# Where the row-chunk sums of layer 0's modulation vectors 2 to 5 are taken: VectorE accumulators in place of TensorE products

## The chip, the core and the metric

The kernel runs on one core of a Trainium2 chip (trn2). Its engines work side by side, each through its own queue in order: TensorE (PE; PEld is its weight load) multiplies 128x128 blocks into PSUM, VectorE (DVE) and ScalarE (ACT) work on tiles of 128 partitions, GpSimd (POOL) does a few small operations, and SyncE (SP) issues nearly all loads. The metric is device microseconds of one execution; the median of three runs before the change is 2529.5 us.

## The reference, cut to what matters

Two transformer layers and a second block work on 512 tokens of 1024 features; layer 0 also carries 256 context tokens. Each layer is modulated by six vectors that come from the conditions c (tokens) and c_ctx (context):

```python
silu_c = jax.nn.silu(c)
silu_cc = jax.nn.silu(c_ctx)
for layer in range(DEPTH):
    mod_x = jnp.split((silu_c @ ada_w[layer] + ada_b[layer])[:, None, :], 6, axis=-1)
    mod_c = jnp.split((silu_cc @ ada_w[layer] + ada_b[layer])[None, None, :], 6, axis=-1)
    hx = rms_norm(x, norm1_g[layer]) * (1 + mod_x[1]) + mod_x[0]
    ...                                       # the mixer: y_x, y_c
    x = x + mod_x[2] * y_x
    x = x + mod_x[5] * sqrelu_mlp(rms_norm(x, norm2_g[layer]) * (1 + mod_x[4]) + mod_x[3], mlp_w1[layer], mlp_w2[layer])
    ...                                       # the same for the context in layer 0
```

A vector i is thus two rows (for c and c_ctx) times a matrix of 1024 x 1024, 4 MB of ada_w. Vectors 0 and 1 of layer 0 are needed at the start; vector 2 after the mixer, 3 and 4 at the second norm, 5 at the end of the feed-forward.

## The kernel before

Activations lie feature-major, eight chunks of 128 features by 512 tokens, split into two parts hi and lo so that a product of full precision is three matmuls (line 302 in fm, feature-major; line 332 in tm, token-major). A unit of 256 weight columns is loaded on SP (line 262) and split by ScalarE and VectorE (lines 339, 340).

Layer 0 runs so. A start-up with an order written out by hand (to about 76 us) makes vectors 0 and 1 chunk by chunk together with the norm and the first product. Then come two token-major products (to 112 us), the gate scans of the mLSTM on VectorE (lines 748 to 763, whose results TensorE transposes in line 769), eight feature-major products (to 259 us: "the projections"), the mLSTM head by head (259 to about 380 us) and the output product, whose first weights are staged through two tiles named ada (line 245). In the mLSTM TensorE makes scores (lines 852 to 862), ScalarE their exponentials e (line 204), VectorE the products r = scores times e (line 869), and TensorE the outputs from r (line 884); lines 888 to 896 are the short end of a query tile, 901 to 910 that of a head. The scores run three tiles ahead of the outputs of the group before.

Vectors 2 to 5 of layer 0 are mixed into this as "fillers": generators of which pump() takes one step at certain places, one after each of the ten products and two in each group of queries of the mLSTM. ada(l, i) has eight steps for a vector. Each loads 128 rows by 1024 columns of ada_w (512 KB, line 472) into one of two tiles ada and lets line 464 multiply them by the conditions: four matmuls of 32 columns of weights side by side, accumulated in one PSUM tile over the steps. The eighth step ends with ada_end: a copy (line 447), two transposes (line 450) and the bias adds into mods (line 457).

Layer 1 has another generator, ada_v(fp, l, i), mixed into the feed-forward of layer 0. Its eight steps each load two chunks of 128 rows by 512 columns (512 KB, line 489). VectorE multiplies each by the condition's value, a scalar for each partition, and adds it to an accumulator mac of 128 x 512 (line 495 for the first chunk, line 497 for the others), one accumulator for each variant (c, c_ctx) and half of the columns; tag mac has four buffers. After the last chunk line 464 adds up the 128 partitions with the constant pick as weights, one call of four matmuls for each variant, and ada_end follows.

Outside the start-up the order on every engine is set when the program is built, by a planner: of the instructions that its own estimate holds ready, the one that stands first in the program goes first. At run time each queue keeps that order, whatever comes late.

Of the kernel before, what the change touches and what calls it, by code (L numbers as in the profile page):

```python
# [10 lines left out]
F32 = mybir.dt.float32  # L11
# [7 lines left out]
P = 128  # L19
# [32 lines left out]
# buffers: the arena of feature-major tiles, short-lived tiles (two sizes), hidden tiles of the feed-forwards  # L52
N_ARENA, N_TMP, N_TMP1, N_HS = 44, 4, 9, 6
N_H, N_H1, N_H2 = 12, 8, 12
# buffers of the attentions and of the rotation tables of the state space branch
N_AO, N_AP, N_E, N_RING, N_ST, N_SP, N_SW, N_TAB = 4, 12, 8, 16, 4, 12, 9, 8
# PSUM banks for products, elsewhere and in the grouped attention
N_MM, N_MA = 5, 6
# columns of a weight tile that are split at a time
W_S = 528  # L60
# start-up: lags of the first products behind the norm, and of the weights
VLAG, W_AT = 2, 3
# pauses in the steps of a norm (plain norms, modulated norms)
WS, WN = (3, 4), (0, 1)
# mLSTM: tiles the scores run ahead; the group (of the last head) at which the next weights come
N_AHEAD, ML_G = 3, 1
# grouped attention: rotations on GpSimd, slots of the rotations and of the next weights, pauses before a turn,
# order of the start (digit: queries of a unit; t: turn of the keys, r: rotation, p: first head; capital: mixed in)
RG, ROPES, SG_AT, N_Y = ("q",), (-1, -1, 0, 0, 3, 4, 5, 6, 9, 10, 11, 12), 21, 3
AT_ORD = "1ttttrrrr2pppP3"  # L70
# state space branch: steps that go early, and how they are mixed in
SS_M, SS_E, SS_V, N_SS = 2, 4, 2, 1
# stick-breaking attention: heads prepared and scored ahead, slots of the statistics, norms and next weights
N_PRE, SB_E, ST_AT, NORM_AT, SG_SB, PW_T = 1, 1, (1, 4), (2, 4, 6, 7), 4, "sp"
# memory attention: pauses in the steps of the heads and of the keys
# [4 lines left out]
def body(ctx: ExitStack, tc: tile.TileContext, a):  # L80
# [15 lines left out]
    def nm(s):  # L96
        cnt[0] += 1
        return f"{s}{cnt[0]}"

# [1 line left out]
    banks, wts = {}, {}  # L101

    def open_w():
        """the place of the weights, which other things take where no weights come by"""
        es = ExitStack()
        wts["pool"] = pool(es, nm("w"), 2, side="right")
        return es

    def open_psum(mm):
        """the eight PSUM banks: mm for products, the rest for everything else"""  # L110
        es = ExitStack()
        for tag, n in (("mm", mm), ("sp", 8 - mm)):
            banks[tag] = es.enter_context(tc.tile_pool(name=nm("psp"), bufs=n, space=PSUM))
        return es
# [7 lines left out]
    def tt(n=NX, dt=F32):  # L122
        """short-lived [P, n <= 512]"""
        if n <= 256:
            return tmp.tile([P, 256], dt, tag="u", name=nm("u"), bufs=N_TMP1)[:, :n]
        return tmp.tile([P, 512], dt, tag="t", name=nm("t"), bufs=N_TMP)[:, :n]

    def s2(dt=F32, n=NX):
        """[P, n <= 512] that lives until its last use"""
        return arena.tile([P, 512], dt, tag="a", name=nm("a"), bufs=N_ARENA)[:, :n]  # L130
# [5 lines left out]
    def new_x(n, with_ctx):  # L136
        """n feature chunks: a tile of the 512 tokens and, with_ctx, one of the 256 context tokens"""
# [7 lines left out]
    def new_act(n, with_ctx, new=s2):  # L145
        """n feature chunks as (hi, lo) pairs"""
# [41 lines left out]
    # one table set of the scalar engine at a time, in the order of the program  # L188
# [19 lines left out]
    def load_after(x, dst, src):  # L208
        """a load that waits for instruction x, so that it takes its place in memory no sooner"""
# [7 lines left out]
    def pump(n=1):  # L217
        """some steps of the work that waits to be mixed in"""
# [21 lines left out]
    def stage(src):  # L240
        """loads the weights that the next product begins with while their place is taken; returns what splits them"""
# [14 lines left out]
    def load_w(src, kc, ncols):  # L256
        """both parts of a unit of columns, as functions of (chunk of rows, columns)"""
# [12 lines left out]
    def fm(src, kc, act, rngs, evac, c0=0, koff=0, ksplit=None, first=None, last=None, done=None, then=None, steps=1, mix=0, tag="mm"):  # L270
        """feature-major product. rngs: (token tile, start, length, variant). evac(chunk, [(range, psum)]).
        first / last: the ranges of the first / last unit of columns in groups, done(range) after each of the last;
        then: the weights that the next product begins with. ksplit: the order of the rows, in parts, of which the first is
        taken ahead for the columns that begin. mix: a step of other work after every so many rows"""
# [41 lines left out]
    def tm(src, act, tts, evac, steps=1):  # L316
        """token-major product of one unit of columns: evac(token tile, psum [128 tokens, columns]).
        src and evac may be lists, for units that go side by side"""
# [18 lines left out]
    def split(hi, lo, src, ce=A, se=V):  # L337
        """src = hi + lo exactly, both in float32r"""
# [27 lines left out]
    def stat_end(acc, d):  # L366
        """1 / sqrt(mean + eps) of the columns' sums, on all partitions"""
# [22 lines left out]
    def norm_apply(x, rb, g, b, hi, lo):  # L390
        """hi + lo = x * g * rb + b"""
# [14 lines left out]
    def need(t, s, n):  # L406
        """the norms of the tokens that the next product takes"""
# [36 lines left out]
    def ada_end(l, i, p):  # L444
        """modulation vector i of layer l, feature-major, from the products in rows 32 j + variant"""
# [20 lines left out]
    def ada(l, i):  # L466
        """the modulation vectors for c and c_ctx; a step for each chunk of rows"""
        p = None
        for k in range(KC):
            src = a["ada_w"][l, k * P:(k + 1) * P, i * 1024:(i + 1) * 1024]  # L470
            st = tmp.tile([P, 1024], F32, tag="ada", name=nm("ada"), bufs=2)
            nc.sync.dma_start(st, src)
            if p is None:
                p = ps()[:, :256]
            ada_rows(p, sc[:, k, :], lambda j: st[:, j * 256:(j + 1) * 256], k == 0, k == KC - 1)
            if k < KC - 1:
                yield
        ada_end(l, i, p)
        yield

    def ada_v(fp, l, i):
        """the same with the sums over the chunks of rows taken by the vector engine"""
# [32 lines left out]
    def norm_late(X, act, acc, g):  # L515
        """act = x * g at once; 1 / sqrt(mean + eps) comes later, as rc (tokens on partitions) and rb (along the tokens),
        and the products are multiplied by it. Returns put(chunk, start, length),
        done(range), ready(start, length) and the two"""
# [61 lines left out]
    # ================= layer 0: mLSTM || short conv =================  # L580
# [17 lines left out]
    # the first two modulation vectors by feature chunks, each with its norm and its share of the first products  # L598
# [100 lines left out]
    fillers += [ada(0, i) for i in range(2, 6)]  # L699
# [15 lines left out]
    # gates: g = ig - cumsum(log f), running maximum, in rows per (direction, head)  # L715
# [30 lines left out]
    def scan2(dst, d0, d1, op0, op1, init):  # L746
        """along ctx then x (forward rows); along reversed ctx then reversed x (backward rows)"""
# [16 lines left out]
    # per key tile: g in columns 0, 1 (direction); exponent of the guard in columns 2, 3  # L764
# [9 lines left out]
    # short conv  # L774
# [25 lines left out]
    # q, k  # L800
# [25 lines left out]
    # mLSTM, a head at a time; three groups of 256 queries (the last: the context), key tiles in pairs  # L826
# [14 lines left out]
    def ml_scores(h, g, PT):  # L841
# [4 lines left out]
        for a_ in ((4, same, 2 - same) if g < 2 else (4,)):  # L846
# [6 lines left out]
            for d in ((0, 1) if a_ in (4, same) else ((1,) if g == 0 else (0,))):  # L853
                # minus the running maximum of the queries, on all partitions, and the triangle
# [43 lines left out]
    def ml_end(h):  # L898
        """the norm of a head and its turn to feature-major, in steps"""
# [14 lines left out]
    # the scores of a group run some tiles ahead of the outputs of the group before it  # L914
# [57 lines left out]
    def norm_spill(r):  # L972
        """the last residual of layer 0: its norm, and the copy that waits in memory"""
# [10 lines left out]
    # ================= layer 1: grouped attention =================  # L984
# [37 lines left out]
    # rotation tables with the gains of the norms  # L1022
# [49 lines left out]
    # keys, both parts stacked on partitions; and the upper part with a row of ones  # L1072
# [31 lines left out]
    def at_prep(c, st):  # L1104
        """queries of pair c as (upper part twice, lower part and -max): a step for each slot of the products"""
# [35 lines left out]
    def at_score(c, e, i):  # L1141
        """exp(scores - max), keys of tile i on partitions"""
# [9 lines left out]
    def at_end(c, o, sums):  # L1152
        """divide by the sums: a step for each slot"""
# [122 lines left out]
    # ================= second block =================  # L1276
# [8 lines left out]
    def rot_table(t):  # L1285
        """cosine and sine of state tile t at all times"""
# [17 lines left out]
    def ssm_consts():  # L1304
        """what depends on the weights alone: decay, rotation, B and C as stationary operands"""
# [4 lines left out]
        def expm1_into(dst, y, tmpn):  # L1310
            """exp(y) - 1: Taylor series of y / 128, seven doublings"""
# [22 lines left out]
        # sines and cosines of theta * 2**s, s = -1 .. 8  # L1334
# [6 lines left out]
        def wrap(x):  # L1341
            """x - 2 pi round(x / 2 pi)"""
# [13 lines left out]
        # (a - 1) and its imaginary part; the factor of B  # L1356
# [145 lines left out]
    # the gated input of the convolution, padded on the left  # L1502
# [25 lines left out]
    def conv():  # L1528
        """31 taps in eight products of four; 32 channels on partitions in four copies, each a token on, and four such side by side"""
# [73 lines left out]
    # what hides the keys that are not before the query: [own tile | next], [tile before | own]  # L1603
# [502 lines left out]
```

## Time and profile before

| what | value |
|---|---|
| median of the runs | 2529.5 us (2528.23 to 2531.26, 3 runs) |
| span of the profiled execution | 2529.6 us |
| busy: PE, PEld, DVE, ACT, POOL | 2472.5, 2011.5, 1505.4, 916.8, 119.4 us |
| granted clock of TensorE over the span | 0.993 |
| busy of 122 us, projections (137 to 259 us) | PE 122.0, DVE 37.2 |
| busy of 104 us, mLSTM (259 to 363 us) | PE 102.4, DVE 55.0 |

The span is counted from the first to the last instruction of one profiled execution. A view of groups gives how long a line's instructions were busy and what ended the idle time before them. The chain of waits is followed back from the last instruction: what stands on it set the end. [...]

### The profile page before, as it was taken

What the parts mean: (1) busy time and instruction counts of PE and PEld (TensorE: products, weight loads), DVE (VectorE), ACT (ScalarE), POOL (GpSimd) and SP (SyncE); (2) the same over time, 40 slices, a digit from 0 to 9 for tenths busy, and PEclk for the clock granted to TensorE, in tenths of its full rate; (3) what the DMA queues carried; (4) which work ended last, traced back from release to release, by engine and by line L of the source; (5) the groups of instructions that cost most, each with busy time, mean ns of one, the idle gap of its engine ahead of it and who ended that gap; (6) DMA issues with size and microseconds to landing.
All of it is one profiled execution on the core that took longest, in us unless ns stands there. A gap on an engine that the chain in (4) does not pass through costs nothing.

```text
span 2529.6 us, 34899 instructions
## 1 busy us (share of the span) xinstructions
PE 2472.5 (98%) x13920; PEld 2011.5 (80%) x13920; DVE 1505.4 (60%) x3208; ACT 916.8 (36%) x1942; POOL 119.4 (5%) x172
## 2 busy tenths in 40 slices
PE   7999999999999999999999999999999999999999
PEld 6888779988888889954578888785867978888887
DVE  5433468676553437799777674488568666443442
ACT  4311463322221224456533222342476534322321
POOL 0000110000000000143200000000000000000000
PEclk9999999999999999999999999999999999999999
DMA  8321354235442212100323323333104522223222
GB/s 245 101 92 51 105 162 159 67 127 172 137 130 67 67 64 87 39 1 1 100 71 100 100 84 100 96 103 91 47 1 134 167 67 97 87 73 118 92 78 91
DMA packets 210674, 238.48 MB, mean 94 GB/s; under 512 B 10704, under 2 KB 166992, under 8 KB 210512
## 3 DMA queue, kind: packets, MB, share of 16 engines
q1 hardware_dynamic: 204624, 232.92, 29.2%
q10 hardware_dynamic: 5888, 3.33, 0.4%
q8 instruction: 109, 1.79, 0.3%
q14 instruction: 53, 0.43, 0.1%
HBM read 225.63 MB, written 8.39 MB: 93 GB/s over the span
## 4 chain that ended last, share of the span: by engine, by line
PE 89%; DVE 6%; DMA 2%; ACT 1%; POOL 1%; issue 1%; SPq 1%; ACTq 0%; POOLq 0%; DVEq 0%
PE ps L302 65%; PE ps L332 7%; PE ps L884 2%; PE ps L646 1%; DMA ada<-ada_w 1%; PE ps L1236 1%; PE ps L464 1%; PE ps L852 1%; PE ps L1743 1%; DVE mx L1127 1%; PE ps L1543 1%; PE ps L1146 1%; PE ps L387 1%; SPq L611 1%; PE ps L1126 1%
## 5 line engine op out<-in xcount | busy, mean ns | idle before, releaser
L302 PE MATMUL ps<-a,whi 128*128 128x512 f32 (+1 forms) x3784 | 994.5, 357 | 2.6 <-ACT a L397 1.5
L302 PEld LDWEIGHTS ps<-a,whi 128*128 128x128 f32 x3784 | 640.7, 189 | 121.0 <-issue 7.7
L302 PE MATMUL ps<-a,wlo 128*128 128x512 f32 (+1 forms) x1980 | 643.9, 358 | 0.0
L339 ACT CAST whi<-wst 128x528 fp32r<-128x528 f32 (+3 forms) x611 | 338.1, 610 | 616.6 <-PE ps L302 533.9
L302 PE MATMUL ps<-h,whi 128*128 128x512 f32 (+1 forms) x1776 | 460.3, 355 | 6.8 <-DVE h L339 6.7
L340 DVE TENSOR_TENSOR wlo<-wst,whi 128x528 fp32r<-128x528 f32 (+3 forms) x611 | 390.2, 674 | 88.4 <-ACT whi L339 87.5
L302 PEld LDWEIGHTS ps<-a,wlo 128*128 128x128 f32 x1980 | 345.5, 189 | 60.0 <-issue 2.0
L302 PEld LDWEIGHTS ps<-h,whi 128*128 128x128 f32 x1776 | 296.7, 189 | 59.7 <-DVE h L339 10.2
L302 PE MATMUL ps<-h,wlo 128*128 128x512 f32 (+1 forms) x800 | 239.2, 349 | 0.0
L570 DVE SCALAR_TENSOR_TENSOR a<-ps,mods,a 128x512 f32<-128x512 f32 (+1 forms) x200 | 122.0, 639 | 156.3 <-PE ps L302 156.0
L332 PE MATMUL ps<-whi,a 128*128 128x256 f32 (+1 forms) x1024 | 191.9, 285 | 0.6 <-ACT a L1576 0.6
L332 PEld LDWEIGHTS ps<-whi,a 128*128 128x128 f32 x1024 | 159.6, 188 | 12.1 <-issue 8.4
L302 PEld LDWEIGHTS ps<-h,wlo 128*128 128x128 f32 x800 | 134.2, 189 | 20.4
L332 PE MATMUL ps<-wlo,a 128*128 128x256 f32 (+1 forms) x512 | 145.1, 284 | 0.2 <-DVE wlo L340 0.2
L559 ACT ACTIVATE t<-ps 128x512 f32<-128x512 f32 x60 | 35.9, 598 | 290.0 <-PE ps L302 277.3
L339 DVE CAST h<-t 128x512 fp32r<-128x512 f32 x60 | 25.5, 425 | 148.5 <-ACT t L561 148.4
L332 PEld LDWEIGHTS ps<-wlo,a 128*128 128x128 f32 x512 | 96.3, 188 | 2.0 <-issue 1.4
L497 DVE SCALAR_TENSOR_TENSOR mac<-ada,sc,mac 128x512 f32<-128x512 f32 x112 | 80.8, 746 | 16.9 <-DMA ada<-ada_w 15.8
L344 POOL TENSOR_TENSOR sm<-sm,mhalf 128x2 f32<-128x2 f32 (+2 forms) x27 | 28.5, 1056 | 979.6 <-DVE sm L380 978.8
L204 ACT ACTIVATE p<-ps 128x512 f32<-128x512 f32 x96 | 53.6, 596 | 41.1 <-PE ps L1147 35.6
L1127 DVE TENSOR_REDUCE mx<-ps 128x1 f32<-128x512 f32 (+1 forms) x128 | 62.8, 546 | 6.0 <-PE ps L1126 5.7
L1991 DVE TENSOR_TENSOR a<-a,ps 128x512 f32<-128x512 f32 x16 | 11.0, 687 | 84.2 <-PE ps L302 84.2
(432 smaller groups left out, 2988.1 us busy)
## 6 DMA issues: line engine op xcount, KB each, us to landing
wst<-mlp_w SPq DMA_DIRECT2D x64, 1024.0 KB, 5.3
ada<-ada_w SPq DMA_DIRECT2D x80, 512.0 KB, 4.0
wst<-ffn_w_in SPq DMA_DIRECT2D x20, 1024.0 KB, 5.3
wst<-ffn_w_out SPq DMA_DIRECT2D x16, 704.0 KB, 4.5
wst<-hyb_w_in SPq DMA_DIRECT2D x10, 1024.0 KB, 5.4
wst<-w_in SPq DMA_DIRECT2D x9, 1024.0 KB, 5.4
a<-ada_w SPq DMA_DIRECT2D x32, 256.0 KB, 6.1
wst<-att_w_in SPq DMA_DIRECT2D x6, 1024.0 KB, 5.5
```

Of the source, the lines that this page charges most:

```text
L204: i = A.activation(out, in_, func, **kw)
L302: T.matmul(p, w(k, slice(m, m + P)), tiles[t][i // 2][:, s:s + n], start=(k == k0 and i == 0), stop=(k == k1 and i == 2))
L332: T.matmul(p, tiles[i // 2][:, s:s + P], (wl if i == 1 else wh)(k, slice(0, n)), start=(k == 0 and i == 0), stop=(k == KC - 1 and i == 2))
L339: last["copy"] = (ce.copy if ce is A else ce.tensor_copy)(hi, src)
L340: return se.tensor_tensor(lo, src, f(hi), ALU.subtract)
L344: G.tensor_tensor(r, v, mhalf[:, :n], ALU.pow)
L387: T.matmul(p, ones, dg, start=True, stop=True)
L497: V.scalar_tensor_tensor(m, x, s, m, op0=ALU.mult, op1=ALU.add)
L559: A.activation(r, p, AF.Relu)
L570: V.scalar_tensor_tensor(xs, p, mod(l, 5)(c, v), xs, op0=ALU.mult, op1=ALU.add)
L884: T.matmul(o, x, VS[:, kt, h, :], start=(n_ == 0), stop=(n_ == len(terms) - 1))
L1127: V.tensor_reduce(MX[:, e, t, i:i + 1], z, AX.X, ALU.max)
```

## The change

The fillers of layer 0 are made by ada_v in place of ada, and ada goes. Vectors 2 to 5 then have the same eight steps at the same places, but each step loads two chunks of 512 columns instead of one of 1024, VectorE does four operations of 128 x 512 (two chunks, two variants) instead of TensorE's four matmuls, and TensorE sums over the partitions once for each vector and variant. The accumulators take four tiles of 128 x 512 in the pool "mlv", which the mLSTM's values share. All else in the diff is comments and docstrings that are left out.

```diff
-    def ada(l, i):
-        p = None
-        for k in range(KC):
-            src = a["ada_w"][l, k * P:(k + 1) * P, i * 1024:(i + 1) * 1024]
-            st = tmp.tile([P, 1024], F32, tag="ada", name=nm("ada"), bufs=2)
-            nc.sync.dma_start(st, src)
-            if p is None:
-                p = ps()[:, :256]
-            ada_rows(p, sc[:, k, :], lambda j: st[:, j * 256:(j + 1) * 256], k == 0, k == KC - 1)
-            if k < KC - 1:
-                yield
-        ada_end(l, i, p)
-        yield
...
-    fillers += [ada(0, i) for i in range(2, 6)]
+    fillers += [ada_v(fp, 0, i) for i in range(2, 6)]
```

## Rows read from the trace of the kernel before

**Rows 1.** The page: span, and the chain's shares by engine.

```profile
span 2529.6 us, 34899 instructions
...
PE 89%; DVE 6%; DMA 2%; ACT 1%; POOL 1%; issue 1%; SPq 1%; ACTq 0%; POOLq 0%; DVEq 0%
```

**Rows 2.** Chain of waits, projections: start us, us, what.

```profile
224.08 0.57 PE ps L464 x8
```

**Rows 3.** Chain of waits, 259 to 363 us: shares by line; pieces.

```profile
by line: PE ps L884 31.7%; PE ps L852 23.1%; PE ps L464 16.2%; PE ps L857 10.4%; PE ps L862 4.9%; DMA ada<-ada_w 4.6%; PE ps L861 2.5%; PE ps L910 2.3%; PE ps L450 1.0%; ACT a L339 0.8%; issue 0.6%; ACT e L204 0.5%; ACT u L892 0.4%; PE ps L
...
274.69 0.55 PE ps L464 x2
...
275.66 0.56 PE ps L464 x6
```

**Rows 4.** Windows: stretch, us; busy us (count) PE, PEld, DVE, ACT, POOL; clock, DMA, GB/s.

```profile
137.00:259.00 122.00, 122.00 (x731) 103.82 (x730) 37.16 (x72) 18.40 (x37) 1.05 (x2) 1.00 0.21 65
259.00:283.00 24.00, 23.18 (x142) 15.93 (x141) 11.08 (x29) 11.73 (x38) 1.25 (x3) 0.86 0.37 110
283.00:363.00 80.00, 79.24 (x610) 61.23 (x609) 43.91 (x123) 49.57 (x170) 11.85 (x21) 1.00 0.40 120
363.00:381.00 18.00, 16.73 (x117) 15.06 (x116) 14.04 (x39) 9.73 (x35) 4.50 (x5) 1.00 0.88 289
...
400.00:458.00 58.00, 57.57 (x417) 54.40 (x417) 51.82 (x111) 22.70 (x48) 2.19 (x3) 1.00 0.30 91
```

**Rows 5.** Tile mac, layer 1: ns min/median/max, first and last start; its idle time.

```profile
L497 DVE SCALAR_TENSOR_TENSOR mac<-ada,sc,mac x112: 731/746/754, 374.9 to 747.4; 128x512 f32<-128x512 f32 x112
...
L495 DVE TENSOR_SCALAR mac<-ada,sc x16: 476/480/489, 373.5 to 737.1; 128x512 f32<-128x512 f32 x16
...
  DMA ada<-ada_w: 23.2, 14
```

**Rows 6.** Timeline of VectorE, 376 to 470 us: start, us, instructions.

```profile
400.35 4.72 DVE L497 SCALAR_TENSOR_TENSOR mac<-ada,sc,mac 128x512 f32<-128x512 f32 x7
```

**Rows 7.** Timeline of SP's DMA issues, 20 to 870 us.

```profile
352.99 4.31 SPq L245 DMA_DIRECT2D ada<-hyb_w_out  x2
...
431.75 0.37 SPq L489 DMA_DIRECT2D ada<-ada_w  x1
...
514.48 3.02 SPq L489 DMA_DIRECT2D ada<-ada_w  x2
```

**Rows 8.** Line 464 in layer 1, as rows 5.

```profile
L464 PE MATMUL ps<-mac,pick x64: 379/379/403, 510.8 to 855.4; 128*32 128x256 f32 x64
```

**Rows 9.** Timeline of VectorE, 60 to 140 us.

```profile
73.20 2.56 DVE L340 TENSOR_TENSOR wlo<-wst,whi 128x528 fp32r<-128x528 f32 x4 [5.24 <-ACT whi L339]
```

**Rows 10.** Timeline of TensorE, 40 to 80 us.

```profile
75.90 0.28 PE L332 MATMUL ps<-whi,a 128*128 128x264 f32 x1
```

**Rows 11.** Who waited for whom, 60 to 140 us: total, times, longest.

```profile
PE ps L769 <- DVE a L761: 4.2, 1, 4.2
```

**Rows 12.** The page's DMA issues: count, KB each, us to landing.

```profile
ada<-ada_w SPq DMA_DIRECT2D x80, 512.0 KB, 4.0
```

**Rows 13.** Chain of waits at the mLSTM's tail.

```profile
375.03 0.65 DVE mac L497
...
380.56 39.54 PE ps L302 x228
```

**Rows 14.** Groups of VectorE, 363 to 381 us: busy, mean ns, idle before.

```profile
L497 DVE SCALAR_TENSOR_TENSOR mac<-ada,sc,mac 128x512 f32<-128x512 f32 x4 | 3.0, 739 | 0.0
```

**Rows 15.** Groups of VectorE, 259 to 363 us.

```profile
L869 DVE TENSOR_TENSOR r<-ps,e 128x512 f32<-128x512 f32 x45 | 30.8, 689 | 20.7 <-ACT e L204 20.3
```

**Rows 16.** Who waited for whom, TensorE, 570 to 640 us.

```profile
PE ps L302 <- DVE h L339: 3.6, 2, 2.6
```

**Rows 17.** Chain of waits, 560 to 640 us.

```profile
587.22 7.11 DMA ada<-ada_w
```

**Rows 18.** Tile mods, 255 to 470 us, as rows 5.

```profile
L457 DVE TENSOR_TENSOR mods<-ps,cols x6: 154/158/166, 288.7 to 360.6; 128x8 f32<-128x8 f32 x6
```

## The prediction

> **What bounds the kernel now.** I read the page first: TensorE is busy in 98% of a span of 2529.6 us and carries 89% of the chain that ended last [rows 1]. So an edit that takes matmuls away can pay microsecond for microsecond, if what replaces them stays off the chain. Then I read the chain in the two stages where vectors 2 to 5 are made. In the projections, 137 to 259 us, it is TensorE without a hole; a step of the old generator stands as eight short records of 0.57 us between runs of the projections' own matmuls [rows 2]. In the mLSTM, 259 to 363 us, line 464 has 16.2% of the chain: 16.8 us of 104 [rows 3]. There a step is often torn apart (two records, other work, then six), and each piece costs about 0.55 us again [rows 3]: the planner drops single matmuls of a step into holes. Third, the table of windows for VectorE: 37.2 us busy of 122 in the projections, 11.1 of 24 at the start of the mLSTM, 43.9 of 80 in the rest of it, 14.0 of 18 at its tail; 51.8 of 58 (89%) in the following stage, with TensorE still at 57.6 of 58 [rows 4]. Last, the groups of layer 1, where the new generator already runs.
>
> The profiled execution's span is 2529.6 us and the median of the three times 2529.5 us; I add the sum to 2529.5. Under 0.2% (5.1 us) counts as no change, about what a measurement of this kernel can tell.
>
> **What is removed from TensorE.** 32 steps, nine before 259 us and 23 in the mLSTM. The nine cost 9 x 0.57 = 5.1 us [rows 2], the 23 cost 16.8 us [rows 3], together 21.9. Added are eight calls of the same four matmuls, two for each vector, with the accumulators as data: 8 x 0.57 = 4.6 us. Net 17.3 us less TensorE on the chain: 4.0 before 259 us and 13.3 after. That is all there is to win. A stall goes too: in the mLSTM the matmuls no longer wait for a load of ada, VectorE waits in their place.
>
> **What is added on VectorE.** For each vector 4 TENSOR_SCALAR and 28 SCALAR_TENSOR_TENSOR of 128x512: by the durations in layer 1 (0.48 and 0.746 us) 22.8 us [rows 5]; back to back seven of them took 4.72 us, 0.674 each [rows 6], which gives 28 x 0.674 + 4 x 0.435 (a TENSOR_SCALAR shortened as much) = 20.6 us. Four vectors: 82 to 91 us. The transposes, bias adds and the number of loads (32 of 512 KB) stay as they were; a load now brings two chunks of 512 columns.
>
> [...]
>
> **Where they lie.** Two rules can be read from layer 1. Sums run ahead of their place in the program, as soon as data and VectorE are free; and they stop until the vector before is finished, since the four accumulators come free only with its matmuls with pick, which TensorE runs at their place: after the load issued at 431.75 the next one of ada stands at 514.48, behind the first such matmul at 510.8 [rows 7, 8]. Applied here:
>
> Vector 2 has its first two loads early; its 20.6 us fit into VectorE's idle time before the gate scans. Its matmuls stand where its eighth step stood, at 224 us [rows 2]. Two spots are tight. The weights of the first product after the start-up are split at 73.2 us and used at 75.9 us [rows 9, 10]: a sum that waits for its load ahead of them in VectorE's queue costs what exceeds some 2 us. And TensorE waits 4.2 us for the scans' last results [rows 11]; a sum between the scans adds 0.7 us each. Neither is shown by this trace: 0 to 3 us each. I take 1 for both together.
>
> Vector 3 may run from about 221 us, when VectorE is a third busy. With two buffers, a load of 4.0 us [rows 12] and 2.7 us of sums, a step takes (4.0 + 2.7)/2 = 3.4 us, eight some 27 us: done by 249 us, before the mLSTM begins at 259 - 4 = 255 us. Cost nothing; its cover is the idle VectorE.
>
> Vectors 4 and 5 fall into the mLSTM, and there the cover is thin. From 259 us to 380.6, where the next product has TensorE to itself [rows 13], VectorE works 11.1 + 43.9 + 14.0 = 69.0 us [rows 4], of which four sums of layer 1 and two first products, 3.0 + 2 x 0.48 = 4.0, can wait [rows 5, 14]: 65 us. Two vectors add 41 to 46. Together 106 to 111 us of work, while TensorE's own stage shrinks from 121.6 to 108.3 us. So **VectorE becomes the limit of this stage**. It is never denser than the 89% of 400 to 458 us [rows 4]; at that density the stage takes 119 to 125 us, from 255 to 374 to 380, against 380.6 before: 0.6 to 6.6 us earlier, if the sums of vector 4 can start as the stage starts. They can if the matmuls that end vector 3 slip into a hole at the stage's start, as the torn steps do [rows 3]. Queued behind a sum are r (line 869: 45 products that scores and outputs wait for, itself idle 20.3 us for ScalarE's e [rows 15]) and the short operations of a head's end; at the tail a sum of layer 1 stands on the chain already, with 0.65 us [rows 13].
>
> **The wait that is added** is that of VectorE for a load. In layer 1 its sums waited 23.2 us for ada in 14 places [rows 5], over 48 steps: 0.48 us a step. Behind such a wait stood h, and TensorE lost 3.6 us in two places [rows 16]; there a load showed on the chain for 7.1 us [rows 17]. Over the 16 steps of vectors 4 and 5 that is 0 to 7.7 us; the density taken above holds part of it, and I take 3. The staged weights of the next product need the two ada buffers back: their loads stood at 352.99 [rows 7], and come later now if vector 5 is late. Bounds 0 to 4 us, I take 1, since the first half of that product only fills holes. Sum: -3.6 (middle of -6.6 and -0.6) + 1 + 3 + 1 = +1.4 us, **about 2531 us**; with all the bounds of these costs at the likely place -6 to +8.
>
> **Rivals.** (1) *Hidden after all*: the scores run some tiles ahead, r tolerates the delay, and VectorE is packed denser than 89%, or part of vector 5 passes the mLSTM's end without holding anything. Then most of the 17.3 us stays: -10 to -17, some 2516 us. For it: TensorE lost 0.4 us in 58 with VectorE at 89% [rows 4]. Against it: 106 us of work in 108 us leave no slack, and r is in a chain of engines that hand over to each other. (2) *Vector 4 is held at its place*: the matmuls ending vector 3 wait for their program place (its bias add stood at 288.7 us [rows 18], now some 281). Until then VectorE does only its old 11.1 us, and 54 + 41 to 46 us remain: at 89% 107 to 112 us, so the stage ends at 388 to 393, 7 to 12 us later than before; with the waits of loads +8 to +20, some 2543 us: **slower**. It decides at whether that call of line 464 runs before or after about 270 us. [...] (3) *It does not do what it says*: another order of everything falls out of the planner and eats or gives some us elsewhere, near 2530 us.
>
> **How the numbers follow.** Chances: forecast 0.46, hidden 0.18, held at its place 0.32, other order 0.04. The predicted time is 2531 us, own range 2524 to 2538. Low end 2516, in the middle of the first rival; high end 2546, which leaves out the upper third of the second: some 0.1 beyond each. Faster by over 0.2% (below 2524.4): 0.18 and an eighth of the forecast, 0.24. Slower (above 2534.6): nearly all of 0.32 and a seventh of the forecast, 0.37. Within: 0.39.
>
> **What would show it.** Line 464 falls from 320 matmul records to 128, 64 for each layer. The period of the projections falls from 17.4 to 16.8 us. Ada loads bunch, with a pause before about 221 us. In the mLSTM VectorE's share must rise to near 90%, its idle time must be put down to ada and to e, and TensorE must show waits for r. If TensorE stays near 99% there, rival 1 holds; if VectorE idles until 281 us and the stage then drags past 385, rival 2. The forecast is wrong in kind if the start-up or the scans lose more than 3 us each, or if the stages behind 381 us, which I count as unchanged, move.

## The result and the profile after

The changed kernel takes **2553.9 us** (median of four, 2552.95 to 2555.95) against 2528.9 us for the kernel before beside it: a ratio of 1.0096, with an interval of 1.0082 to 1.0111. It is slower, by more than the prediction's range allowed. The profiled executions differ by 22.7 us of span; these are the lines that answer to [rows 1]:

```profile
span 2552.3 us, 34627 instructions
...
PE 86%; DVE 8%; DMA 2%; ACT 2%; SPq 1%; issue 1%; POOL 1%; ACTq 0%; POOLq 0%; DVEq 0%
```

The chain of waits of the kernel after (start us, us, what), cut to the places where stages begin and end, tells where those 22.7 us arose:

```profile
34.65 6.21 DMA ada<-ada_w
40.89 0.88 DVE mac L480 x2
...
60.51 5.49 DMA ada<-ada_w
...
81.87 8.79 PE ps L631 x71
90.66 34.83 PE ps L332 x288
...
140.13 1.09 PE ps L754 x4
...
143.13 91.50 PE ps L302 x520
234.63 1.00 PE ps L464 x16
...
236.63 32.61 PE ps L302 x188
...
292.73 1.00 PE ps L464 x16
...
315.18 1.98 DVE mac L482 x3
317.16 1.80 DVE r L854 x3
...
319.71 0.85 ACT e L204 x2
...
382.19 1.95 PE ps L464 x12
...
405.26 14.93 PE ps L302 x86
```

Set against the same marks before, with each stage's own length:

| stage, and the mark that ends it | before, us | after, us | longer by |
|---|---|---|---|
| start-up, to the first token-major product (L332) | 76.06 | 90.66 | +14.6 |
| that product and the scans, to the transposes (L769, now L754) | 50.2, to 126.30 | 49.5, to 140.13 | -0.8 |
| projections, to their last product | 132.8, to 259.1 | 129.1, to 269.2 | -3.7 |
| mLSTM, to the next product alone on TensorE (L302) | 121.5, to 380.56 | 136.0, to 405.26 | +14.6 |
| the rest | 2149.0 | 2147.0 | -2.0 |

So two stages lose 14.6 us each, and the gain that was forecast without doubt, 4.0 us ahead of the mLSTM, came as 3.7 in the projections and 0.8 before them.

**The start-up.** VectorE's timeline (start, us, instructions, idle time before and what ended it) shows how it begins:

```profile
40.89 0.88 DVE L480 TENSOR_SCALAR mac<-ada,sc 128x512 f32<-128x512 f32 x2 [10.15 <-DMA ada<-ada_w]
41.69 0.74 DVE L482 SCALAR_TENSOR_TENSOR mac<-ada,sc,mac 128x512 f32<-128x512 f32 x1
42.35 0.48 DVE L398 SCALAR_TENSOR_TENSOR a<-u,mods,a 128x256 fp32r<-128x256 f32 x1
```

The first sum of vector 2 stands in VectorE's queue ahead of the norm's modulation (L398), and its load is issued at 34.65 us, as the first of ada was in the kernel before. VectorE waits 10.15 us for it, and the norm, whose data was there, waits behind. From 36 to 91 us VectorE is then busy for 44.8 of 55 us, with all 32 sums of vector 2 among the norm's steps. TensorE's last matmuls of the start-up follow VectorE's last splits, at 81.87 us.

**The mLSTM.** The table of windows, columns as in [rows 4], gives the stages and then the mLSTM in pieces, behind the mLSTM of the kernel before in a fence of its own:

```profile
259.00:381.00 122.00, 119.15 (x863) 92.22 (x862) 69.03 (x190) 71.03 (x241) 17.59 (x28) 0.97 0.46 143
```

```profile
36.00:91.00 55.00, 43.87 (x428) 41.32 (x424) 44.80 (x96) 18.16 (x41) 0.00 (x0) 0.91 0.68 198
143.00:269.00 126.00, 126.00 (x730) 110.16 (x730) 58.82 (x108) 19.04 (x40) 1.05 (x2) 0.99 0.26 76
269.00:406.00 137.00, 120.99 (x723) 96.71 (x723) 106.25 (x254) 71.61 (x241) 24.24 (x28) 0.88 0.32 96
...
269.00:293.00 24.00, 22.95 (x124) 18.29 (x127) 12.01 (x32) 12.88 (x42) 1.37 (x3) 0.79 0.00 1
293.00:317.00 24.00, 23.29 (x162) 19.59 (x155) 19.92 (x48) 15.34 (x53) 4.05 (x6) 0.93 0.22 66
317.00:341.00 24.00, 19.40 (x127) 15.27 (x126) 20.26 (x48) 10.96 (x40) 6.00 (x5) 0.93 0.38 111
341.00:365.00 24.00, 21.78 (x142) 17.16 (x141) 21.57 (x49) 14.11 (x48) 4.03 (x5) 1.00 0.31 88
365.00:390.00 25.00, 19.58 (x87) 14.04 (x85) 19.45 (x45) 10.42 (x33) 3.94 (x4) 0.66 0.36 106
390.00:406.00 16.00, 13.98 (x95) 12.37 (x96) 13.04 (x36) 7.91 (x29) 4.86 (x5) 1.00 0.83 262
```

In the first 24 us VectorE does 12.0 us of work and no load of ada moves (DMA 0.00): the four accumulators are taken until the matmuls with pick that end vector 3, and these run at 292.73 us, 23.5 us into the stage, although the last sum of vector 3 starts at 262.9 us. From there to the end VectorE is busy 78 to 90% of each piece. TensorE, which had 119.15 of 122 us in this stage before, idles 16 of 137, and its granted clock, a share of full speed, is 0.88 against 0.97. The same matmuls of scores and outputs, 600 in both kernels, also take longer: the busy times of their five groups add up to 106.9 us before and 119.6 after, and a matmul of the largest group of scores takes 328 ns on average against 304. Who waited for whom there (us in total, times, longest), TensorE first:

```profile
PE ps L842 <- DVE r L854: 2.9, 3, 2.2
PE ps L837 <- ACT e L204: 2.2, 4, 0.9
PE ps L464 <- DVE mac L482: 2.1, 2, 1.8
PE ps L842 <- ACT e L204: 1.7, 2, 0.9
...
DVE r L854 <- ACT e L204: 9.9, 10, 2.2
```

On the chain at 315 us three sums stand directly ahead of three r, and two e come soon after. r waits behind sums in VectorE's queue, and scores wait for r and for e. Of the 9.9 us that r itself waits for e, 9.6 lie in the first 24 us. The groups of VectorE from 269 to 406 us say what fills it, and that the loads hardly held it:

```profile
L482 DVE SCALAR_TENSOR_TENSOR mac<-ada,sc,mac 128x512 f32<-128x512 f32 x61 | 44.6, 753 | 0.2 <-DMA ada<-ada_w 0.2
L854 DVE TENSOR_TENSOR r<-ps,e 128x512 f32<-128x512 f32 x48 | 31.9, 684 | 10.2 <-ACT e L204 9.9
L480 DVE TENSOR_SCALAR mac<-ada,sc 128x512 f32<-128x512 f32 x10 | 4.7, 478 | 0.8 <-PE ps L464 0.8
```

### The profile page after: what moved, and what is told of

The parts are those of the page before. It is cut to its first block, busy times and chain, and to the rows that moved or that the text cites. A ratio compares the mean times of both kernels' runs of the same rounds, so it can differ in the third digit from the quotient of the medians.

```text
span 2552.3 us, 34627 instructions
## 1 busy us (share of the span) xinstructions
PE 2473.8 (97%) x13728; PEld 2018.6 (79%) x13728; DVE 1581.8 (62%) x3336; ACT 917.5 (36%) x1942; POOL 126.0 (5%) x172
## 4 chain that ended last, share of the span: by engine, by line
PE 86%; DVE 8%; DMA 2%; ACT 2%; SPq 1%; issue 1%; POOL 1%; ACTq 0%; POOLq 0%; DVEq 0%
PE ps L302 64%; PE ps L332 7%; PE ps L869 1%; DMA ada<-ada_w 1%; DVE mac L482 1%; PE ps L1221 1%; PE ps L837 1%; SPq L596 1%; PE ps L1728 1%; DVE mx L1112 1%; PE ps L1528 1%; PE ps L1131 1%; PE ps L387 1%; PE ps L1111 1%; PE ps L1439 1%
## 5 line engine op out<-in xcount | busy, mean ns | idle before, releaser
L302 PE MATMUL ps<-a,whi 128*128 128x512 f32 (+1 forms) x3784 | 992.5, 357 | 2.6 <-ACT a L397 1.6
L302 PEld LDWEIGHTS ps<-a,whi 128*128 128x128 f32 x3784 | 641.0, 189 | 118.7 <-issue 5.2
L302 PE MATMUL ps<-a,wlo 128*128 128x512 f32 (+1 forms) x1980 | 644.6, 359 | 0.0
L302 PE MATMUL ps<-h,whi 128*128 128x512 f32 (+1 forms) x1776 | 458.8, 354 | 5.0 <-DVE h L339 4.9
L302 PEld LDWEIGHTS ps<-a,wlo 128*128 128x128 f32 x1980 | 345.8, 189 | 59.9 <-issue 1.9
L302 PEld LDWEIGHTS ps<-h,whi 128*128 128x128 f32 x1776 | 295.7, 188 | 57.7 <-DVE h L339 8.4
L302 PE MATMUL ps<-h,wlo 128*128 128x512 f32 (+1 forms) x800 | 238.7, 349 | 0.0
L332 PE MATMUL ps<-whi,a 128*128 128x256 f32 (+1 forms) x1024 | 191.7, 285 | 0.6 <-ACT a L1561 0.6
L482 DVE SCALAR_TENSOR_TENSOR mac<-ada,sc,mac 128x512 f32<-128x512 f32 x224 | 161.3, 750 | 18.2 <-DMA ada<-ada_w 17.0
L332 PEld LDWEIGHTS ps<-whi,a 128*128 128x128 f32 x1024 | 159.5, 188 | 11.7 <-issue 8.4
L302 PEld LDWEIGHTS ps<-h,wlo 128*128 128x128 f32 x800 | 133.9, 188 | 20.3
L332 PE MATMUL ps<-wlo,a 128*128 128x256 f32 (+1 forms) x512 | 145.2, 285 | 0.2 <-DVE wlo L340 0.2
L332 PEld LDWEIGHTS ps<-wlo,a 128*128 128x128 f32 x512 | 96.2, 188 | 2.0 <-issue 1.4
```

What stands on the lines that cost most here:

```text
L302: T.matmul(p, w(k, slice(m, m + P)), tiles[t][i // 2][:, s:s + n], start=(k == k0 and i == 0), stop=(k == k1 and i == 2))
L332: T.matmul(p, tiles[i // 2][:, s:s + P], (wl if i == 1 else wh)(k, slice(0, n)), start=(k == 0 and i == 0), stop=(k == KC - 1 and i == 2))
L482: V.scalar_tensor_tensor(m, x, s, m, op0=ALU.mult, op1=ALU.add)
```

## The experiments

Theory: the start-up is late because a sum waits at the head of VectorE's queue for a load, and the mLSTM is long because the sums of vectors 4 and 5 stand in it, held until vector 3's matmuls with pick. Rivals: in the start-up the work of 32 sums and not the wait; in the mLSTM the number of sums alone, their loads, or TensorE without steps to fill its holes. All results first. The ratio is against the runs of the kernel before beside each kernel (medians 2528.6 to 2529.9 us); the marks are read as in the table above, the first L332 by its first record.

| kernel | median us (lowest to highest) | ratio to before, interval | first L332 | projections end | mLSTM, us |
|---|---|---|---|---|---|
| before | 2528.9 | | 75.9 | 259.1 | 121.5 |
| after | 2553.9 (2553.0 to 2556.0) | 1.0096, 1.0082 to 1.0111 | 90.5 | 269.2 | 136.0 |
| e8_probe_wait | 2544.5 (2542.7 to 2548.4) | 1.0063, 1.0045 to 1.0080 | 84.7 | 269.9 | 118.3 |
| e1_vector2_only | 2535.3 (2533.0 to 2539.0) | 1.0022, 1.0013 to 1.0031 | 89.5 | 268.8 | 118.2 |
| e2_vectors3to5 | 2543.1 (2539.4 to 2546.8) | 1.0060, 1.0040 to 1.0080 | 75.2 | 258.6 | 132.0 |
| e3_sums_after_startup | 2544.5 (2534.3 to 2549.3) | 1.0056, 1.0037 to 1.0075 | 75.6 | 254.5 | 136.8 |
| e6_half_columns | 2528.6 (2520.8 to 2532.3) | 0.9992, 0.9980 to 1.0003 | 79.0 | 256.6 | 124.2 |
| e5_two_sets | 2518.8 (2513.9 to 2519.9) | 0.9957, 0.9943 to 0.9971 | 76.1 | 255.0 | 116.2 |
| e4_early_places | 2517.7 (2512.3 to 2518.6) | 0.9951, 0.9939 to 0.9964 | 75.2 | 258.3 | 110.1 |
| e4p_early_places_tensor | 2553.9 (2552.1 to 2557.8) | 1.0105, 1.0089 to 1.0120 | 76.8 | 290.8 | 109.7 |
| e7_early_two_sets | 2517.2 (2515.0 to 2520.0) | 0.9955, 0.9942 to 0.9969 | 75.7 | 258.5 | 109.8 |
| e9_early_places_unheld | 2532.4 (2529.7 to 2536.6) | 1.0013, 1.0004 to 1.0022 | 90.2 | 272.2 | 112.6 |
| e10_blank_steps | 2523.8 (2522.2 to 2527.2) | 0.9977, 0.9968 to 0.9987 | 75.8 | 259.3 | 116.2 |

**The two halves of the change.** e1 makes vector 2 on VectorE and vectors 3 to 5 on TensorE; e2 the other way round.

```diff
-    fillers += [ada_v(fp, 0, i) for i in range(2, 6)]
+    fillers += [ada_v(fp, 0, 2)] + [ada(0, i) for i in range(3, 6)]
```

> Vector 2 alone gets its sums on VectorE, vectors 3 to 5 stay on TensorE as in the kernel before. Theory (two separate costs: the sums of vector 2 stand in VectorE's start-up queue and cost some 14 us there; the sums of vectors 4 and 5 cost some 14 us in the mLSTM): the first token-major product starts near 90 us as in the changed kernel (76 before), the mLSTM takes its old 121 us, time about 2539 us. Rival (the start-up's delay is made good later, the mLSTM alone costs): about 2527 us.

> Vector 2 stays on TensorE, vectors 3 to 5 get their sums on VectorE. Theory of two costs: start-up as before (first token-major product at 76 us), mLSTM to the next product 135 us as in the changed kernel against 121 before, time about 2541 us. Rival (the mLSTM's length in the changed kernel is only a sequel of the late start): about 2526 us.

The halves fall apart in the marks. With vector 2 alone the first product starts at 89.5 us, as in the kernel after, and the mLSTM takes 118.2 us. With vectors 3 to 5 alone the start-up is that of before (75.2) and the mLSTM takes 132.0 us. In e1 the loss shrinks from 13.6 us at the first product to 5.6 in the time, since the projections and the mLSTM are shorter by 4 and 3 us. The times therefore do not add up to the whole: 5.6 us in e1 and 13.4 in e2 make 19.0 of the 25.0.

**The start-up: wait or work.** e8 is the kernel before with one copy of 128x1 on VectorE that reads the first tile of vector 2, at the place in the program of the first sum. Nothing else uses the copy.

```diff
             ada_rows(p, sc[:, k, :], lambda j: st[:, j * 256:(j + 1) * 256], k == 0, k == KC - 1)
+            if (i, k) == (2, 0):
+                V.tensor_copy(const.tile([P, 1], F32, name='probe'), st[:, :1])
```

> The kernel before plus one VectorE copy of 128x1 that reads the first loaded tile of vector 2; it stands in VectorE's order where the changed kernel has its first sum, in the start-up. If the start-up's loss is the wait for that load at the head of VectorE's queue: VectorE idles some 10 us there, the first product starts at 85 to 87 us, time about 2538 us. If the loss is the work of the sums between the start-up's instructions: no change, 2529 us.

VectorE's timeline in e8:

```profile
30.82 0.48 DVE L393 SCALAR_TENSOR_TENSOR u<-a,G,a 128x256 f32<-128x256 f32 x1
40.38 0.15 DVE L477 COPY probe<-ada 128x1 f32<-128x1 f32 x1 [9.08 <-DMA ada<-ada_w]
40.45 0.47 DVE L398 SCALAR_TENSOR_TENSOR a<-u,mods,a 128x256 fp32r<-128x256 f32 x1
```

0.15 us of work holds VectorE for 9.08 us, and the first product comes 8.8 us later than before. That is the wait by itself. The kernel after loses 14.6 us there, so the other 5.8 us belong to what it has more of: about 1 us of longer wait and the sums that then stand between the norm's steps. The whole of e8 is 14.8 us above the kernel before beside it, more than those 8.8 and more than the 2538 us expected; the surplus builds up behind the mLSTM. I found no wait there that goes back to the copy, and its cause stays open.

e3 keeps the sums and takes them out of the start-up: the first sum of each accumulator of layer 0 is ordered behind VectorE's last split of the start-up.

```diff
-                split(*(x[:, c - VLAG - 1] for x in (w2[1][1], w2[1][2], w2[1][0])))
+                last["start"] = split(*(x[:, c - VLAG - 1] for x in (w2[1][1], w2[1][2], w2[1][0])))
...
-                            V.tensor_scalar(m, x, s, None, ALU.mult)
+                            y = V.tensor_scalar(m, x, s, None, ALU.mult)
+                            if l == 0:
+                                after_(y, last["start"])
```

> The changed kernel, with one more edge of order: the first sums of an accumulator of layer 0 come after the last VectorE instruction of the start-up. Theory of two costs: the start-up's 14 us come back, the mLSTM stays long, about 2539 us. Rival (sums anywhere before the projections cost the same, in front of the first product's weight splits): about 2550 us.

The first product starts at 75.6 us, the projections end at 254.5, 4.6 us ahead of the kernel before, and all of that and nearly 11 us more are lost in the mLSTM (136.8 us). The time, 2544.5 us, is 5 us above the 2539 of the theory. Its runs scatter over 15 us, so its median says less than its marks.

**The mLSTM: gate or amount.** e5 is e3 with eight accumulators in layer 0 in place of four; e6 is e3 with the sums of vectors 4 and 5 over half the columns.

```diff
-            accs.append([fp.tile([P, 512], F32, tag="mac", name=nm("mac"), bufs=4) for _ in vs])
+            accs.append([fp.tile([P, 512], F32, tag="mac", name=nm("mac"), bufs=8 if l == 0 else 4) for _ in vs])
```

> e3 with eight accumulators in layer 0 and not four, so that the sums of a vector no longer wait for the matmuls with pick of the one before. If the late start of vector 4 (held until 23 us into the mLSTM) stretches it, 15 to 16 of its sums move into the projections and the first 24 us of the mLSTM: the mLSTM takes 119 to 128 us and not 136.8, and the time is 2528 to 2537 us. If the sums stretch it by their number wherever they stand in it, or by the starved TensorE, it stays at 133 us or more and 2540 to 2545 us.

```diff
+                        n = 256 if l == 0 and i > 3 else 512
-                        x, m, s = st[:, k * 512:(k + 1) * 512], accs[h][v], sc[:, k0 + k, v:v + 1]
+                        x, m, s = st[:, k * 512:k * 512 + n], accs[h][v][:, :n], sc[:, k0 + k, v:v + 1]
```

> e3 with the sums of vectors 4 and 5 over 256 of each 512 columns (the other half of these two vectors is left out of the computation; the matmuls with pick read the first half twice); loads, order and gate stay. VectorE's work in the mLSTM falls by some 18 us of 105. If VectorE's work is the limit from vector 4's start on, the mLSTM shortens by 12 to 18 us to 119 to 125, and the time is 2526 to 2533 us. If it is the gate, the loads or the number of instructions in the queue, less than 5 us: 2539 us or more.

The windows of the whole mLSTM in e3, e6 and e5, one fence for each:

```profile
254.00:391.00 137.00, 120.92 (x718) 96.89 (x717) 105.31 (x253) 70.56 (x239) 24.25 (x28) 0.86 0.31 94
```

```profile
256.00:381.00 125.00, 118.61 (x722) 96.89 (x721) 89.84 (x254) 70.58 (x240) 19.86 (x28) 0.88 0.35 105
```

```profile
255.00:372.00 117.00, 113.84 (x729) 94.46 (x730) 86.36 (x223) 70.40 (x242) 21.04 (x28) 0.93 0.25 76
```

Both answers are yes, and they fit one mechanism. e6 keeps the gate, the loads and the number of instructions (x254 against x253) and takes 15.5 us of VectorE's work out: the stage shortens by 12.6 us. e5 keeps every sum and moves a vector's worth ahead of the gate: 19 us less of VectorE's work in the stage, and it shortens by 20.6, which is more than was expected of it (2518.8 us against 2528 to 2537). VectorE's work behind the gate set the end. Neither the count of instructions nor the loads did. TensorE's clock did not make the difference between e3 and e6 either: it is 0.86 and 0.88 in these windows, the busy times of the groups of scores and outputs add up to 120.5 us in e3 and 119.6 in e6, and their waits shrink, as the largest group of scores shows, e3 first (busy us, mean ns, idle before):

```profile
L839 PE MATMUL ps<-a,a 64*128 64x256 f32 x168 | 34.1, 329 | 3.1 <-ACT e L204 2.6 <-DVE r L856 0.4
```

```profile
L840 PE MATMUL ps<-a,a 64*128 64x256 f32 x168 | 33.7, 326 | 1.4 <-DVE r L857 0.8 <-ACT sm L876 0.6
```

In e5 the sum is 116.0 us at a clock of 0.93, so of its 20.6 us a part of up to 4.5 can be the clock's.

**The place alone.** e4 is e3 with the ten projections taking three or four steps of the waiting work each in place of one (the expectation below says 2, but the kernel has one), so that nothing of layer 0 is left for the mLSTM; e4p does the same to the kernel before, whose sums are on TensorE.

```diff
-    tm(w_in[:, 1024 + 264:1024 + 528], get, TT_, ev_o1)
+    tm(w_in[:, 1024 + 264:1024 + 528], get, TT_, ev_o1, steps=3)
...
-        fm(w_in[:, 2576 + 256 * h:2832 + 256 * h], KC, get, FXC, ev_u)
+        fm(w_in[:, 2576 + 256 * h:2832 + 256 * h], KC, get, FXC, ev_u, steps=4)
```

> e3 (first sum behind VectorE's last instruction of the start-up) with one more size changed: the ten projections take 3 or 4 steps of the waiting work each in place of 2, so that all 32 steps, their sums and their matmuls with pick stand before the mLSTM. Theory (in e3 the mLSTM, 136.8 us against 121.5, is stretched by the sums of vectors 4 and 5 that stand in it): the mLSTM falls below 121.5 us, since the steps that TensorE did there are gone too; 121.5 less 16.8 of line 464 is 105, so with 4 x 0.57 more in the projections some 2529.7 - 17 = 2513 us, at most 2520 if VectorE waits for loads in the projections. Rival (the mLSTM is stretched for another reason, such as TensorE's missing filler work and a lower clock): it stays at 130 us or more and the time at 2535 to 2545.

> The kernel before (sums on TensorE), with the ten projections taking 3 or 4 steps each as in e4_early_places: the place alone, without the engine. The 23 steps that stood in the mLSTM now cost 0.57 us each in the projections. If TensorE is full in either place, nothing moves: 2529.7 less (16.8 - 23 x 0.57 = 3.7) is 2526 us at best. If the holes of the mLSTM can't be filled otherwise, the mLSTM loses less than 16.8 us and the time rises to 2535. If it falls to 2520 or below, the gain of e4_early_places would be that of the place and not of VectorE.

In both the mLSTM falls to 110 us. But the same place costs nothing on VectorE (projections end at 258.3) and 32 us on TensorE (290.8), and e4p, at 2553.9 us, lies far above the 2520 to 2535 that were expected. About 13 of the 32 us are the matmuls of the 23 steps themselves (23 x 0.57). Who waited in e4p between 75 and 291 us, TensorE:

```profile
PE ps L464 <- DMA ada<-ada_w: 9.2, 7, 2.6
```

Seven loads of ada stand on e4p's chain there with 3.8 to 4.0 us each, of which TensorE filled all but 9.2 us with other matmuls. What makes up the other 10 us of the 32 is not separated. In e4p a step on TensorE that came sooner than its load stopped the projections behind it, for 9.2 us in seven places; on VectorE the sums of e4 waited 6.8 us for loads in six places, and TensorE shows no wait for them in the projections. That is the good side of the edit, and e4, at 2517.7 us, is faster than both kernels.

> e4 (early places, first sum behind the start-up) with the eight accumulators of e5. In e4 the mLSTM took 110.2 us and no sum of layer 0 is left in it, so a second set has only the projections to help, and there TensorE is already without a hole (132.0 of 132 us). Theory: no change against e4, 2515 to 2520 us. Rival (the gate still delays something in e4): 2505 to 2512 us.

e7 puts the eight accumulators into e4 and changes nothing (2517.2): once no sum is left in the mLSTM there is no gate to open.

> The changed kernel with early places alone: as e4, but the first sum of vector 2 is again free to go anywhere in VectorE's queue. If the two losses add up, the start-up is late by the 14.6 us that it is in the changed kernel and the mLSTM short as in e4: 2517.7 + 14.6 = 2532 us. If sums that are done early in the start-up are worth something later (the projections of the changed kernel took 3.5 us less than before), it is some 2526 to 2529 us.

e9 is e4 without the order edge of e3. It costs 14.7 us against e4, with the first product again at 90.2 us, so the loss of the start-up comes on top in full.

**What ate the rest of the gain.** e4 gains 11.0 us, not the 17.3 of matmuls that it sheds. e10 puts steps back that do no work: the four matmuls of a step on a constant tile, 29 times, without load and without sums.

```diff
+    blank = cols[:, :256]
...
+    def idle_steps(n):
+        for k in range(n):
+            if k % 8 == 0:
+                p = ps()[:, :256]
+            ada_rows(p, pick[:, 0, :], lambda j: blank, k % 8 == 0, k % 8 == 7 or k == n - 1)
...
+    fillers.append(idle_steps(29))
```

> e4_early_places with 29 more steps of the same four matmuls on constants already in memory, whose result is used by nobody: six of them fall into the projections (6 x 0.57 = 3.4 us later) and 23 into the mLSTM, at the places where TensorE's steps stood in the kernel before. No load and no VectorE work comes with them. Theory (without small steps in its holes TensorE gets a lower clock in the mLSTM: 0.93 in three stretches and 0.83 in the fourth of e4, against 1.00 in the kernel before): the granted clock comes back to 0.97 or more over the mLSTM, which takes 118 to 121.5 us in place of 110.2, and not 110.2 + 23 x 0.61 = 124; the time is 2528 to 2532 us. Rival (the clock there has nothing to do with the steps): it stays at 0.93 or below, the mLSTM takes 123 us or more, and the time is 2534 us or more.

Four pieces of the mLSTM in e4, and then in e10:

```profile
258.00:282.00 24.00, 22.71 (x137) 18.79 (x136) 13.44 (x35) 15.39 (x50) 1.83 (x4) 0.93 0.00 1
282.00:306.00 24.00, 23.69 (x159) 20.67 (x158) 13.88 (x40) 15.32 (x56) 4.07 (x7) 0.93 0.00 1
306.00:330.00 24.00, 23.70 (x159) 20.69 (x158) 13.94 (x40) 15.54 (x58) 4.06 (x7) 0.93 0.00 1
330.00:350.00 20.00, 19.65 (x118) 17.25 (x117) 12.24 (x34) 12.61 (x47) 3.15 (x5) 0.83 0.03 4
```

```profile
259.00:283.00 24.00, 24.00 (x200) 17.21 (x200) 12.67 (x34) 14.37 (x47) 1.83 (x4) 1.00 0.00 1
283.00:307.00 24.00, 24.00 (x187) 18.95 (x186) 13.17 (x37) 14.18 (x51) 3.61 (x6) 1.00 0.01 1
307.00:331.00 24.00, 24.00 (x187) 18.85 (x185) 13.74 (x37) 15.21 (x53) 3.61 (x6) 1.00 0.00 1
331.00:351.00 20.00, 20.00 (x161) 15.16 (x162) 10.36 (x31) 12.14 (x43) 3.61 (x6) 1.00 0.00 1
```

Of the 29 blank steps, 27 fell into the mLSTM (216 matmul records of line 464 there, eight to a step) and not 23. They are 27 x 0.57 = 15.4 us of matmuls, and the stage is only 6.1 us longer (116.2 against 110.1), as the time is (2523.8 against 2517.7). The clock came back as the theory had it, but stage and time are shorter than its ranges. The granted clock is 1.00 in all four pieces with them and 0.83 to 0.93 without, in pieces where TensorE was busy 95 to 99% without them and all the time with them. (In the kernel before, which the expectation puts at 1.00, it was 0.86 in the first 24 us and 1.00 from there on [rows 4].) The mean scores matmul (line 839 in e4, 852 in e10) takes 296 ns with the blank steps and 315 without; the busy times of the five large groups of the stage, equal in number in both, add up to 103.2 us with them and 112.0 without. So the 9.3 us that the blank steps don't cost come from two places: shorter matmuls at the higher clock, and holes that they fill (TensorE idles 2.25 of 92 us in e4's four pieces and 0.0 of 92 in e10's). The groups overlap (the 112.0 us lie in 105.5 us in which TensorE is busy, from 258 to 369 us), so how much each gives is not separated here. Together they mean that, by this measure, matmuls taken out of this mLSTM give back 40% of what they took.

## Why the prediction was wrong

**The steps that held.** Line 464 has 64 records left in layer 0 as in layer 1. The sums take 746 ns and 482 ns (medians of 117 and 18 in the first 410 us of the trace after), as in [rows 5]. In the projections vector 3 was free: TensorE is busy for 126.0 of 126 us and the stages ahead of the mLSTM are 4.5 us shorter, against 4.0 forecast. The wait for the scans, [rows 11], is 4.0 us; no sum stood between the scans, since vector 2 was done by 83.5 us and vector 3 was held until the matmuls at 234.63.

**The step that failed first: "its 20.6 us fit into VectorE's idle time before the gate scans", with 0 to 3 us at each of two tight spots, 1 taken for both.** It measured 14.6, and the prediction itself had named more than 3 us there as the sign that it was wrong in kind. I looked for the danger at the splits of 73 us [rows 9] and counted the sums as work for idle time. But VectorE's idle time in the start-up of before is no room: from 30 to 78 us 13.4 us of it lie in 14 places of at most 2.0, each a wait for ScalarE's half of a norm step, and the first load of ada is issued only at 34.56 us. A sum placed ahead of the norm's next step waits until the load has landed, and e8 shows that a copy of 0.15 us costs 8.8 us there. That vector 2 "has its first two loads early" was true of their place in the program and not of the time at which they land. The bound had to be: landing of the load less the place of the first sum, some 10 us, and up to the 20.6 us of sums behind it.

**The step that failed second: the mLSTM, at -3.6 us, by 89% of density from its first microsecond.** The -3.6 holds 4.0 us won ahead of the stage; the stage itself was to take 119 to 125 us from 255 us on, and took 136.0. The condition named there, that the matmuls ending vector 3 slip into a hole at the stage's start, did not come true; they ran at their place, 292.73 us, 23.5 us into the stage. So the second rival held: it puts 107 to 112 us behind the gate, and from 292.73 to 405.26 us it was 112.5. That the figure fits so closely is partly luck. VectorE had 94.2 us of work there and not 95 to 100, and was busy for 83% of the 113 us and not for 89%. Nor is 89% the most it reaches: in the kernel before it was busy for 60.0 of 63 us from 1075 us on. The waits that kept it at 83% were not those for e, but mostly for ScalarE in the short ends of the query tiles (us in total, times, longest, from 293 to 406 us):

```profile
DVE sm L874 <- ACT sm L873: 5.8, 9, 1.7
DVE u L878 <- ACT u L877: 5.5, 9, 1.0
...
DVE r L854 <- ACT e L204: 0.3, 1, 0.3
```

e5 and e6 show that the gate and the work behind it are the cause, each in its own way. TensorE's own matmuls may have added to it: at a clock of 0.88 against 0.97 the busy times of scores and outputs rose by 12.7 us against the kernel before, and how much of that reached the end of the stage is not separated.

**Terms that were off with little effect.** Waits for loads in the mLSTM: 3 us taken, 0.2 us measured: VectorE is late in this stage, and its loads are not. The staged weights of the next product were loaded at 374.77 us against 352.99 before [rows 7], but TensorE's waits in this stage name no load. The stages behind 381 us, counted as unchanged, gave 2.0 us back.

**The sum.** With the second rival's 2543 us and 13.6 us more for the start-up one comes to 2557; less the 3 us for loads that weren't waited for, 2554. That it meets the 2553.9 is in part luck, since the spans of the two profiled executions differ by 22.7 us and the medians by 25.0. The range ended at 2546 because it left out the upper third of the rival's price, and because that price held at most a few us for the start-up.

**And the first rival.** That "most of the 17.3 us stays" happens only in e4, e5 and e7, at 2517 to 2519 us, and there by taking the sums out of the start-up and all of them, or in e5 a vector's worth, out of the mLSTM, not by packing them denser.

## What to carry to other kernels

Work that goes to an idle engine is to be priced at two points before its length counts: what stands behind its first instruction in that engine's queue, and when that instruction's data lands; here 0.15 us of work cost 8.8. Where few accumulators tie one vector's sums to the end of the vector before, divide the work by the time behind that gate, and give the sums an earlier place or a second set; with the start-up kept free, either made a loss of 25 us a gain of 10 to 11. The same early place for matmuls that wait for loads cost 25 us, so here the change of engine had to come with the change of place.

## What the hardware showed beyond that

TensorE's granted clock fell where small matmuls were taken out of a stage that stayed 95 to 99% busy: 0.93, 0.93, 0.93 and 0.83 in the four pieces of e4, against 1.00 in each of those of e10 with 27 idle steps. The engine's longest wait between 258 and 369 us of e4 was 2.0 us. What in these stretches lets the clock fall is not shown by these runs; that it was 1.00 with the holes filled is, and also that this filling doesn't pay here: it costs 6.1 us more than it returns.
